# Thirty-two tiles in place of thirty-three for the routed experts of a decoder block, with other fixed experts

## The chip, the core and the metric

The kernel runs on one core of one Trainium2 chip. The metric is the device time of one execution, in microseconds (us). The core has a matrix engine (PE, with its weight loads as PEld), a vector engine (DVE), a scalar engine (ACT), a general engine (POOL) and SyncE (SP), which here issues nearly all transfers (DMAs). PSUM is the memory that PE writes.

## What is computed

One layer of a decoder block on 512 tokens of width 1024, in float32: two attention mixers with gates and an output projection, and behind them a mixture of 64 experts (each 1024 to 256 to 1024, SwiGLU), six experts for each token, and one shared expert. The part that matters here:

```python
_, expert_idx = lax.top_k(jnp.where(expert_keep, choice, NEG_INF), TOP_K)      # 6 of 64 for each token
def expert_block(xs):
    tok, g, e = xs
    xb = x_pad[tok]
    hb = jax.nn.silu(xb @ w_exp_gate[e]) * (xb @ w_exp_up[e])
    return (hb @ w_exp_down[e]) * g[:, None]
routed = jax.ops.segment_sum(yb.reshape(n_rows, D), row_tok, num_segments=T + 1)[:T]
shared = (jax.nn.silu(xf @ w_sh_gate) * (xf @ w_sh_up)) @ w_sh_down
return (shared + routed).reshape(B, S, D)
```

512 tokens with six experts each are 3072 rows of work for the 64 experts. How many an expert gets is known only once the router has run; for the inputs used it lies between 12 and 98.

## The kernel before

**Up to the router.** The norms, the projections, the two attentions, the merge and the output projection fill the first half of the span. The weights of four routed experts whose number is fixed beforehand (experts 0 to 3, `E0 = 4`) and of the shared expert are loaded in that time. `route`, `place` and `scatter` write for each expert a list of its tokens into a table in device memory. Then the experts other than the fixed four are ranked by how many rows they have (`krow`, `kcol` and `rowk` are the keys; the fixed ones get a large number added so that they rank first, in order of their number), and `sched` holds the expert of each rank.

**Units and tiles.** A rank has a fixed room of so many units of 32 rows, listed in `UNITS`; an expert with more rows than its rank's room goes into a loop at the very end (`For_i` over `n_over`), which does not run for these inputs. `make_layout` packs the units into tiles of four units, which is 128 rows: 132 units in 33 tiles before. An entry (q) of the layout is an expert in the order of use; it may straddle two tiles. The fixed experts have three units each and share tiles 0 to 3 with one small expert each; tile 31 has four experts and a piece, tile 32 four of one unit each.

**The work of one tile T** on PE, in the order written by hand: `first` (name `gu`, line 1266 before) multiplies the 128 rows by the gate and up weights of each expert of the tile, in halves of 64 rows where all pieces are even, else in quarters of 32 rows; `turn` (`tp`, line 1253) transposes the gathered rows of a later tile; `turn_hidden` (`tp<-hid`, line 1281); `expert_out` (`y`, line 1298) multiplies by the down weights; `combine` (`o`, lines 1322 and 1323) adds the rows to the tokens' sums `acc` through a matrix of zeros and ones, for two tiles at a time. The order in the loop is gate and up of tile T+1, transpose of tile T+2, combine of a finished pair where there is one, down of tile T. With 33 tiles the first combine takes tile 0 alone, with 32 the first one takes tiles 0 and 1.

**The queue of transfers.** There are six slots for an expert's weights: gate and up together as `gu`, down as `dn`, three transfers of 1024 KB. SP issues in program order and waits at each transfer until its slot is free. `tile_ents(T)` is called two tiles ahead of the down of T and asks for the slots' lists (`load_slots`, `tb`, nine entries ahead), the gate and up of each expert of the tile (`load_gu`), and behind each of them the down of the expert two entries earlier (`next_dn`, `DLAG = 2`). `fetch` on POOL gathers the rows of a tile (`xg`, `hs`) by its list. For the last tile the gate and up come as asked for and the downs last, in half pieces.

**The entry** into this stage is the string `ENTRY`: e, g, u and d load an expert's number, gate, up and down, s its list, f gathers a tile.

Of the kernel before, what the change touches and what calls it, by code (L numbers as in the profile page):

```python
# [10 lines left out]
F32 = mybir.dt.float32  # L11
# [6 lines left out]
ALU = mybir.AluOpType  # L18
# [20 lines left out]
EARLY = 1  # L39
SPL = (4, 7)  # L40
PW = {0: 3, 1: 3}
ENTRY = "e1 g1 u1 d1 s0 s1 f0 s2 s3 f1 s4 s5 s6 s7 s8 e3 g3 u3"
BYACT, HALVES = 1, 2
MODS, GST, MODE = 2, 8, ["vvvvvvvv"] * 4

# [1 line left out]

E0 = 4  # L50
UNITS = [3] * E0 + [4] + [3] * 9 + [2] * 39 + [1] * 11


def make_layout():
    small = [r for r in range(E0, 64) if UNITS[r] == 1]
    big = [r for r in range(E0, 64) if UNITS[r] > 2]
    mid = [r for r in range(E0, 64) if UNITS[r] == 2]
    head = [r for e in range(E0) for r in (e, small.pop(0))]
    spread = []
    for group in (big, mid):  # L60
        spread += [((i + 0.5) / len(group), r) for i, r in enumerate(group)]
    ranks = head + [r for _, r in sorted(spread)] + small
    layout, at = [], 0
    for r in ranks:
        pieces, left = [], UNITS[r]
        while left:
            n = min(left, 4 - at % 4)
            pieces.append((at // 4, at % 4, n, UNITS[r] - left))
            at, left = at + n, left - n
        layout.append((r, pieces))  # L70
    assert at % 4 == 0
    return layout, at // 4


LAYOUT, TILES = make_layout()
# [12 lines left out]
def build(ctx, tc, a, out, dbg=None):  # L88
# [594 lines left out]
    late = []  # L683
# [18 lines left out]
    def load_expert(slot, e, parts=1, now=True, after=None):  # L702
        gu = slots[slot][0].tile([128, 2, KD, 256], F32, name="gu", tag=f"gu{slot}")
        dn = slots[slot][1].tile([128, 2, D], F32, name="dn", tag=f"dn{slot}")
        if e is None:
            for j, n in enumerate(("w_sh_gate", "w_sh_up")):
                SP.dma_start(gu[:, j], a[n][0].rearrange("(p k) f -> p k f", k=KD))
            SP.dma_start(dn, a["w_sh_down"][0].rearrange("(b p) n -> p b n", p=128))
            return gu, dn
        moves = []  # L710
        if after is not None:
            for to in (gu[0:1, 0, 0, 0:1], gu[0:1, 1, 0, 0:1], dn[0:1, 0, 0:1]):
                A.copy(to, after[0:1, 0:1])
        for k in range(0, KD, KD // parts):
            for j, src in enumerate((wegv, weuv)):
                v = src[e].rearrange("o (p k) f -> (o p) k f", k=KD)
                moves.append((gu[:, j, k:k + KD // parts], v[:, k:k + KD // parts]))
        moves.append((dn, wedv[e].rearrange("o (p j) n -> (o p) j n", j=2)))
        for to, src in moves:
            if now:  # L720
                SP.dma_start(to, src)
            else:
                late.append(lambda to=to, src=src: SP.dma_start(to, src))
        return gu, dn
# [55 lines left out]
    ast.close()  # L780
    fst.close()
    slots.append([pool("wpd", 1, side="right")] * 2)
    WT[fixed[0]] = load_expert(2, slice(0, 1), now=False)

    owv = a["w_out"][0].rearrange("(k p) n -> p k n", p=128)
    wpb = pool("wpb", 1, side="right")
# [24 lines left out]
    for b in range(KD):  # L811
# [6 lines left out]
        V.tensor_tensor(gates[0][b], gates[0][b], gates[1][b], ALU.add)  # L818
        for j, (H, L) in enumerate(mg):
            split(H[:, b], L[:, b], gates[0][b][:, j * 256:j * 256 + 256], A, G)  # L820
    WT[fixed[1]] = load_expert(1, slice(1, 2), now=False)
    wst.close()
    omst.close()
    gst.close()
# [131 lines left out]
    def score_sum(i):  # L956
        lg = mm_p.tile([128, S], F32, name="lg", tag="mm")
        PE.matmul(lg[:, :NE], scores[i], pairs, start=True, stop=True)
        sc = rt.tile([128, NE], F32, name="sc", bufs=2)
        A.activation(sc, lg[:, :NE], AF.Exp, scale=-1.0)  # L960
        scores[i] = sc
        return sc
# [108 lines left out]
    for c in (1, 0):  # L1071
        out_raw(c)
        chunks[c] = out_split(c)
    WT[fixed[2]] = load_expert(3, slice(2, 3))
    lo, hi = range(0, 4), range(4, 8)
    norm_rows(0)
    norm_rows(1)
# [31 lines left out]
    shared_in(0, 1, 0, hi)  # L1109


    WT[fixed[3]] = load_expert(4, slice(3, 4), after=score_sum(3))
    SP.dma_start(gfb, bc(modd[5 * D:6 * D]))
    shared_in(0, 1, 1)
    place(2)
# [6 lines left out]

    krow = rt.tile([128, NE], F32, name="krow")
    V.tensor_scalar(krow, iota_e, -1.0, float(NE - 1), op0=ALU.mult, op1=ALU.add)
    V.tensor_scalar(krow[:, 0:E0], krow[:, 0:E0], 1e6, None, op0=ALU.add)
    kcol = rt.tile([128, 1], F32, name="kcol")
    G.tensor_scalar(kcol, ecol, -1.0, float(NE - 1), op0=ALU.mult, op1=ALU.add)
    G.tensor_scalar(kcol[0:E0], kcol[0:E0], 1e6, None, op0=ALU.add)
    cr = tr_p.tile([128, S], F32, name="cr", tag="tr")
    cc = cr[:, NE:]  # L1130
    for i in range(NT):
# [80 lines left out]

    def load_slots(q):
        rank, pieces = LAYOUT[q]
        o = rank * STRIDE if rank < E0 else SP.value_load(sched[0:1, 1, rank:rank + 1], min_val=0,
                                                          max_val=(NE - 1) * STRIDE)
        for T, u, n, r in pieces:
            src = table[o + r * 32:o + (r + n) * 32] if rank < E0 else table[ds(o + r * 32, n * 32)]
            SP.dma_start(tb[u * 32:(u + n) * 32, T], src)
# [131 lines left out]
    for step, q in ((t[0], int(t[1])) for t in ENTRY.split()):  # L1351
# [13 lines left out]
            SP.dma_start(gu[:, j], (wegv, weuv)[j][e].rearrange("o (p k) f -> (o p) k f", k=KD))  # L1365
        elif step == "d":
            WT[q][1] = load_dn(where[q], entry[q][1])
    late.append((3, entry[3][1]))
    follow(G.iota(iota_t, pattern=[[1, S]], base=0, channel_multiplier=0), last[0])

    def turn_next(T, parts):
# [186 lines left out]
```

## Time and profile before

| what | value |
|---|---|
| median of 3 runs | 1053.76 us (1049.55 to 1054.71) |
| the profiled execution's own time | 1039.41 us |
| its span, first to last instruction | 1037.6 us |
| mean granted clock of PE | 0.986 |
| PE busy | 999.0 us (96%) |
| DVE busy | 579.4 us (56%) |
| bytes moved | 285.98 MB, mean 276 GB/s |

The profiled execution is 14.35 us below the median of the runs. A busy PE is not PE at its peak, since ends of matmuls are modelled; its idle time and what ended it are what is to be read. Times in the trace are us from the start of the span. "L1266" is a line of the kernel.

### The profile page before, as it was taken

To read this page: it belongs to the slowest core of one execution; us is meant where nothing else is said; L and a number is where in the kernel's file an instruction comes from. 1 tells how busy PE (TensorE), PEld (TensorE's weight loads), DVE (VectorE), ACT (ScalarE), POOL (GpSimd) and SP (SyncE) were. 2 spreads that over 40 slices of the span, in tenths; PEclk is the share of its full clock that TensorE was granted. 3 is DMA by queue.
4 is the path that set the end of the run, shared out by engine and by line. 5 is a ranking of instruction groups with operands and counts; after the bars stand their busy time and mean duration, and the time that the engine had idled before them with its cause. 6 is when DMAs were issued, how large, how long until landed. Compare 5 with 4: busy or idle time off the path is not lost.

```text
span 1037.6 us, 16324 instructions
## 1 busy us (share of the span) xinstructions
PE 999.0 (96%) x5904; PEld 600.2 (58%) x5904; DVE 579.4 (56%) x1157; ACT 319.1 (31%) x712; POOL 158.3 (15%) x208
## 2 busy tenths in 40 slices
PE   9989999998989999999899999999999999999995
PEld 7778667776756668986334344444344444345442
DVE  4568576466757654595254455454455454445465
ACT  4356553232225532430122212122212122212213
POOL 2242001000031275135200000000000000000001
PEclk9999999999999999999999999999999999999998
DMA  9922104599660277635599999999999999999973
GB/s 296 321 86 65 45 1 155 193 282 271 187 211 21 82 263 236 232 104 227 208 415 415 417 416 371 377 418 412 389 378 374 378 408 417 383 366 418 379 264 143
DMA packets 101347, 285.98 MB, mean 276 GB/s; under 512 B 15121, under 2 KB 61929, under 8 KB 77202
## 3 DMA queue, kind: packets, MB, share of 16 engines
q1 hardware_dynamic: 94146, 270.18, 70.2%
q0 software_dynamic: 5648, 12.63, 3.2%
q10 hardware_dynamic: 1472, 2.11, 0.7%
q8 instruction: 47, 0.77, 0.3%
q14 instruction: 34, 0.28, 0.1%
HBM read 282.33 MB, written 4.66 MB: 277 GB/s over the span
## 4 chain that ended last, share of the span: by engine, by line
PE 79%; DVE 7%; DMA 6%; POOL 3%; issue 2%; ACT 2%; SPq 1%; ACTq 0%; POOLq 0%; DVEq 0%
PE gu L1266 22%; PE y L1298 11%; PE o L151 6%; PE o L1322 6%; PE o L150 6%; PE o L152 6%; PE o L1323 6%; PE tp L1253 3%; PE sp L591 3%; PE oc L615 2%; PE tp L603 2%; POOL table L1027 1%; PE tp L1281 1%; DMA w<-in_w_mod_dram 1%; POOL wL L159 1%
## 5 line engine op out<-in xcount | busy, mean ns | idle before, releaser
L1266 PE MATMUL gu<-gu,xT 128*32 128x512 f32 (+1 forms) x1664 | 233.6, 594 | 0.0
L1266 PEld LDWEIGHTS gu<-gu,xT 128*32 128x32 f32 (+1 forms) x1664 | 69.1, 117 | 150.4 <-issue 137.0
L1298 PE MATMUL y<-dn,hid 128*32 128x512 f32 (+1 forms) x832 | 120.3, 596 | 0.5 <-ACT hid L1282 0.5
L1275 DVE TENSOR_TENSOR hid<-hid,gu 128x256 f32<-128x256 f32 x33 | 13.9, 420 | 164.3 <-ACT hid L1274 164.3
L1322 PE MATMUL o<-yH,oht 128*128 128x512 f32 x260 | 103.9, 400 | 0.7 <-DVE acc L1324 0.7
L1324 DVE TENSOR_TENSOR acc<-acc,o 128x512 f32<-128x512 f32 x140 | 93.2, 683 | 17.3 <-PE o L1323 17.3
L1323 PE MATMUL o<-yL,oht 128*128 128x512 f32 x260 | 101.7, 391 | 0.0
L150 PE MATMUL o<-hH,wH 128*128 128x512 f32 x208 | 83.4, 401 | 1.2 <-ACT gate L473 1.2
L151 PE MATMUL o<-hH,wL 128*128 128x512 f32 x208 | 83.1, 399 | 1.5 <-DVE wL L159 1.4
L152 PE MATMUL o<-hL,wH 128*128 128x512 f32 x208 | 82.5, 396 | 0.0
L156 ACT CAST yH<-ys 128x512 fp32r<-128x512 f32 (+1 forms) x68 | 41.1, 605 | 106.3 <-DVE ys L1302 106.3
L159 DVE TENSOR_TENSOR yL<-ys,yH 128x512 fp32r<-128x512 f32 (+1 forms) x68 | 45.8, 676 | 43.3 <-ACT yH L156 43.2
L1298 PEld LDWEIGHTS y<-dn,hid 128*32 128x32 f32 (+1 forms) x832 | 32.7, 117 | 64.3 <-issue 54.2
L1274 ACT ACTIVATE hid<-gu 128x256 f32<-128x256 f32 x33 | 12.7, 384 | 185.2 <-PE gu L1266 185.2
L1302 DVE SCALAR_TENSOR_TENSOR ys<-y,tb,gmb 128x512 f32<-128x512 f32 (+1 forms) x68 | 49.8, 734 | 27.6 <-PE y L1298 24.2
L1241 POOL DMA_INDIRECT xg<-h2d,tb x22 | 22.2, 1009 | 274.4 <-PE tp L1253 196.8
L1322 PEld LDWEIGHTS o<-yH,oht 128*128 128x128 f32 x260 | 48.8, 188 | 14.9 <-DVE acc L1324 2.6
L1323 PEld LDWEIGHTS o<-yL,oht 128*128 128x128 f32 x260 | 48.9, 188 | 9.5
L919 ACT ACTIVATE xT<-tp,ab 128x128 f32<-128x128 f32 x132 | 49.6, 456 | 14.6 <-PE tp L1253 13.0
L921 DVE TENSOR_SCALAR xT<-tp,ab 128x128 f32<-128x128 f32 x132 | 45.2, 404 | 10.9 <-ACT xT L919 7.4
L150 PEld LDWEIGHTS o<-hH,wH 128*128 128x128 f32 x208 | 39.5, 190 | 13.2 <-issue 1.9
L151 PEld LDWEIGHTS o<-hH,wL 128*128 128x128 f32 x208 | 39.6, 190 | 10.9 <-DVE wL L159 3.0
(386 smaller groups left out, 1669.1 us busy)
## 6 DMA issues: line engine op xcount, KB each, us to landing
gu<-in_w_exp_gate_dram SPq DMA_DIRECT2D x63, 1024.0 KB, 8.6
gu<-in_w_exp_up_dram SPq DMA_DIRECT2D x63, 1024.0 KB, 13.1
dn<-in_w_exp_down_dram SPq DMA_DIRECT2D x60, 1024.0 KB, 10.9
w<-in_w_mod_dram SPq DMA_DIRECT2D x32, 512.0 KB, 3.8
w<-in_w_in_dram SPq DMA_DIRECT2D x13, 1024.0 KB, 8.0
wm<-in_w_mod_dram SPq DMA_DIRECT2D x16, 512.0 KB, 7.1
wraw<-in_w_out_dram SPq DMA_DIRECT2D x12, 512.0 KB
dn<-in_w_exp_down_dram SPq DMA_DIRECT2D x8, 512.0 KB, 8.9
```

The source lines that it names most:

```text
L150: PE.matmul(o, l[0], r[0], start=start, stop=False)
L151: PE.matmul(o, l[1], r[0], start=False, stop=False)
L152: return PE.matmul(o, l[0], r[1], start=False, stop=stop)
L159: return le.tensor_tensor(L, src, f(H), ALU.subtract)
L919: A.activation(out, src, AF.Identity, bias=ab2[:, 1, k:k + 1], scale=ab2[:, 0, k:k + 1])
L921: V.tensor_scalar(out, src, ab2[:, 0, k:k + 1], ab2[:, 1, k:k + 1], op0=ALU.mult, op1=ALU.add)
L1266: last[0] = PE.matmul(gu[lo:lo + n], xT[:, k, lo:lo + n], w[:, :, k], start=(k == 0), stop=(k == KD - 1))
L1298: last[0] = PE.matmul(y[lo:lo + m], hT[:, j, lo:lo + m], w[:, j, c], start=(j == 0), stop=(j == 1))
L1302: V.scalar_tensor_tensor(ys[:, b], y[:, b], f(tb[:, T, 1:2]), gfb[:, c][:, b], op0=ALU.mult, op1=ALU.mult)
L1322: m = PE.matmul(o, oht[:, i * 128:(i + 1) * 128], yH[:, c], start=(q == 0), stop=False)
L1323: PE.matmul(o, oht[:, i * 128:(i + 1) * 128], yL[:, c], start=False, stop=(q == len(state) - 1))
L1324: d = V.tensor_tensor(acc[:, i, c], acc[:, i, c], o, ALU.add)
```

## The change

Three of the four parts stand in tables. `UNITS` gives the four fixed experts two units in place of three, keeps one rank of four units, has ten ranks of three, 37 of two and twelve of one, in sum 128 units. `make_layout` no longer lets an expert straddle tiles: tiles 0 and 1 hold the four fixed experts alone, two each; the others hold two experts of two units, or one of three and one of one; in the middle the one expert of four units has tile 16 alone, and behind it tile 17 holds three experts (two units and twice one). The fixed experts are numbers 4 to 7 (`FIX`), with the keys and addresses that follow from it. `ENTRY` is written anew: entries 4 and 5 are now the first to be loaded behind the ranking, and gate and up of the second stand behind six lists in place of nine. The room of experts 4 to 7 is 64 rows each; they get 63, 52, 41 and 56.

```diff
--- before.py
+++ after.py
@@ -39,7 +39,7 @@
 EARLY = 1
 SPL = (4, 7)
 PW = {0: 3, 1: 3}
-ENTRY = "e1 g1 u1 d1 s0 s1 f0 s2 s3 f1 s4 s5 s6 s7 s8 e3 g3 u3"
+ENTRY = "e4 g4 u4 d4 s0 s1 f0 s2 s3 f1 s4 s5 e5 g5 u5 s6 s7 s8"
 BYACT, HALVES = 1, 2
 MODS, GST, MODE = 2, 8, ["vvvvvvvv"] * 4
 
@@ -47,29 +47,31 @@
 
 
-E0 = 4
-UNITS = [3] * E0 + [4] + [3] * 9 + [2] * 39 + [1] * 11
+
+E0, FIX = 4, 4
+UNITS = [2] * E0 + [4] + [3] * 10 + [2] * 37 + [1] * 12
 
 def make_layout():
-    small = [r for r in range(E0, 64) if UNITS[r] == 1]
-    big = [r for r in range(E0, 64) if UNITS[r] > 2]
-    mid = [r for r in range(E0, 64) if UNITS[r] == 2]
-    head = [r for e in range(E0) for r in (e, small.pop(0))]
-    spread = []
-    for group in (big, mid):
-        spread += [((i + 0.5) / len(group), r) for i, r in enumerate(group)]
-    ranks = head + [r for _, r in sorted(spread)] + small
-    layout, at = [], 0
-    for r in ranks:
-        pieces, left = [], UNITS[r]
-        while left:
-            n = min(left, 4 - at % 4)
-            pieces.append((at // 4, at % 4, n, UNITS[r] - left))
-            at, left = at + n, left - n
-        layout.append((r, pieces))
-    assert at % 4 == 0
-    return layout, at // 4
+    of = lambda n: [r for r in range(E0, 64) if UNITS[r] == n]
+    four, three, two, one = of(4), of(3), of(2), of(1)
+    kinds = [[(r, one.pop(0)) for r in three], [(two[i], two[i + 1]) for i in range(0, len(two) - 1, 2)]]
+
+
+    spread = [tile for _, tile in sorted(((i + 0.5) / len(group), tile) for group in kinds
+                                         for i, tile in enumerate(group))]
+    odd = [tuple(four), (two[-1], one.pop(0), one.pop(0))]
+    half = len(spread) // 2
+    tiles = [(e, e + 1) for e in range(0, E0, 2)] + spread[:half] + odd + spread[half:]
+    assert len([r for t in tiles for r in t]) == 64
+    layout = []
+    for T, ranks in enumerate(tiles):
+        at = 0
+        for r in ranks:
+            layout.append((r, [(T, at, UNITS[r], 0)]))
+            at += UNITS[r]
+        assert at == 4
+    return layout, len(tiles)
 
 LAYOUT, TILES = make_layout()
@@ -780,7 +782,7 @@
     ast.close()
     fst.close()
     slots.append([pool("wpd", 1, side="right")] * 2)
-    WT[fixed[0]] = load_expert(2, slice(0, 1), now=False)
+    WT[fixed[0]] = load_expert(2, slice(FIX + 0, FIX + 1), now=False)
 
     owv = a["w_out"][0].rearrange("(k p) n -> p k n", p=128)
     wpb = pool("wpb", 1, side="right")
@@ -818,7 +820,7 @@
         V.tensor_tensor(gates[0][b], gates[0][b], gates[1][b], ALU.add)
         for j, (H, L) in enumerate(mg):
             split(H[:, b], L[:, b], gates[0][b][:, j * 256:j * 256 + 256], A, G)
-    WT[fixed[1]] = load_expert(1, slice(1, 2), now=False)
+    WT[fixed[1]] = load_expert(1, slice(FIX + 1, FIX + 2), now=False)
     wst.close()
     omst.close()
     gst.close()
@@ -1071,7 +1073,7 @@
     for c in (1, 0):
         out_raw(c)
         chunks[c] = out_split(c)
-    WT[fixed[2]] = load_expert(3, slice(2, 3))
+    WT[fixed[2]] = load_expert(3, slice(FIX + 2, FIX + 3))
     lo, hi = range(0, 4), range(4, 8)
     norm_rows(0)
     norm_rows(1)
@@ -1109,7 +1111,7 @@
     shared_in(0, 1, 0, hi)
 
-    WT[fixed[3]] = load_expert(4, slice(3, 4), after=score_sum(3))
+    WT[fixed[3]] = load_expert(4, slice(FIX + 3, FIX + 4), after=score_sum(3))
     SP.dma_start(gfb, bc(modd[5 * D:6 * D]))
     shared_in(0, 1, 1)
     place(2)
@@ -1122,10 +1124,14 @@
 
     krow = rt.tile([128, NE], F32, name="krow")
     V.tensor_scalar(krow, iota_e, -1.0, float(NE - 1), op0=ALU.mult, op1=ALU.add)
-    V.tensor_scalar(krow[:, 0:E0], krow[:, 0:E0], 1e6, None, op0=ALU.add)
+    V.tensor_scalar(krow[:, FIX:FIX + E0], krow[:, FIX:FIX + E0], 1e6, None, op0=ALU.add)
     kcol = rt.tile([128, 1], F32, name="kcol")
     G.tensor_scalar(kcol, ecol, -1.0, float(NE - 1), op0=ALU.mult, op1=ALU.add)
-    G.tensor_scalar(kcol[0:E0], kcol[0:E0], 1e6, None, op0=ALU.add)
+    kfix = rt.tile([128, 2], F32, name="kfix")
+    G.tensor_scalar(kfix[:, 0:1], ecol, FIX - 0.5, 1e6, op0=ALU.is_gt, op1=ALU.mult)
+    G.tensor_scalar(kfix[:, 1:2], ecol, FIX + E0 - 0.5, None, op0=ALU.is_lt)
+    G.tensor_tensor(kfix[:, 0:1], kfix[:, 0:1], kfix[:, 1:2], ALU.mult)
+    G.tensor_tensor(kcol, kcol, kfix[:, 0:1], ALU.add)
     cr = tr_p.tile([128, S], F32, name="cr", tag="tr")
     cc = cr[:, NE:]
     for i in range(NT):
@@ -1212,7 +1218,7 @@
 
     def load_slots(q):
         rank, pieces = LAYOUT[q]
-        o = rank * STRIDE if rank < E0 else SP.value_load(sched[0:1, 1, rank:rank + 1], min_val=0,
+        o = (FIX + rank) * STRIDE if rank < E0 else SP.value_load(sched[0:1, 1, rank:rank + 1], min_val=0,
                                                           max_val=(NE - 1) * STRIDE)
         for T, u, n, r in pieces:
             src = table[o + r * 32:o + (r + n) * 32] if rank < E0 else table[ds(o + r * 32, n * 32)]
@@ -1365,7 +1371,7 @@
             SP.dma_start(gu[:, j], (wegv, weuv)[j][e].rearrange("o (p k) f -> (o p) k f", k=KD))
         elif step == "d":
             WT[q][1] = load_dn(where[q], entry[q][1])
-    late.append((3, entry[3][1]))
+    late.append((5, entry[5][1]))
     follow(G.iota(iota_t, pattern=[[1, S]], base=0, channel_multiplier=0), last[0])
 
     def turn_next(T, parts):
```

On SP, behind the loads of the first ranked expert: `tb` are the lists, `TENSOR_LOAD sched` reads an expert's number for the next instructions, `gu` is a gate or up transfer. Before, the rows up to the first list of the second tile:

```order
L699 DMA dn<-in_w_exp_down_dram 128x2048
L1219 DMA tb<-table 96x2
L1215 TENSOR_LOAD sched
L1215 ISA x2
L1219 ISA
L1219 DMA tb<-table 32x2
L1219 DMA tb<-table 96x2
```

and now up to the second ranked expert's gate:

```order
L701 DMA dn<-in_w_exp_down_dram 128x2048
L1225 DMA tb<-table 64x2 x4
L1221 TENSOR_LOAD sched
L1221 ISA x2
L1225 ISA
L1225 DMA tb<-table 64x2
L1221 TENSOR_LOAD sched
L1221 ISA x2
L1225 ISA
L1225 DMA tb<-table 64x2
L1364 TENSOR_LOAD sched
L1364 ISA x2
```

The two lists of the first tile now follow each other with no number read between them, and six lists in all, not nine, stand ahead of the second expert.

On PE, from the transpose for tile 2 on: `y` is the down product, `o` the combine. Before:

```order
L1253 MATMUL tp<-ident,hs 128x128 x8
L1298 MATMUL y<-dn,hid 32x512 x16
L1281 MATMUL tp<-ident,hid 128x128 x2
L1266 MATMUL gu<-gu,xT 32x512 x32
L1253 MATMUL tp<-ident,xg_3470 128x128 x8
L1322 MATMUL o<-yH,oht 128x512
L1323 MATMUL o<-yL,oht 128x512
```

and now:

```order
L1259 MATMUL tp<-ident,hs 128x128 x8
L1304 MATMUL y<-dn,hid 64x512 x8
L1287 MATMUL tp<-ident,hid 128x128 x2
L1272 MATMUL gu<-gu,xT 64x512 x16
L1259 MATMUL tp<-ident,xg_3470 128x128 x8
L1304 MATMUL y<-dn,hid 64x512 x8
L1287 MATMUL tp<-ident,hid 128x128 x2
L1272 MATMUL gu<-gu,xT 32x512 x32
L1259 MATMUL tp<-ident,xg_3471 128x128 x8
L1328 MATMUL o<-yH,oht 128x512
L1329 MATMUL o<-yL,oht 128x512
```

The combine of tile 0 alone is gone; the next tile's down and gate and up stand in its place, and the first combine takes two tiles.

## Rows read from the trace of the kernel before

**Rows 1.** The page: the span in 40 equal slices of 25.9 us.

```profile
DMA  9922104599660277635599999999999999999973
GB/s 296 321 86 65 45 1 155 193 282 271 187 211 21 82 263 236 232 104 227 208 415 415 417 416 371 377 418 412 389 378 374 378 408 417 383 366 418 379 264 143
```

**Rows 2.** Waits of PE from 500 to 1005 us: total, times, longest.

```profile
PE tp L1281 <- DVE hid L1275: 1.5, 1, 1.5
PE o L1322 <- DVE acc L1324: 0.7, 1, 0.7
```

**Rows 3.** Stretches: length, PE, PEld, DVE, ACT, POOL busy, clock, DMA share, GB/s.

```profile
526.00:976.00 450.00, 449.34 (x2864) 206.56 (x2858) 223.95 (x409) 101.51 (x233) 32.54 (x54) 1.00 0.98 397
526.00:635.00 109.00, 108.34 (x664) 49.74 (x658) 55.20 (x101) 24.62 (x57) 8.43 (x14) 1.00 1.02 416
573.00:588.50 15.50, 15.50 (x86) 5.35 (x80) 6.86 (x12) 4.65 (x10) 1.21 (x2) 1.00 1.02 418
526.50:542.00 15.50, 14.84 (x112) 6.37 (x112) 9.05 (x17) 3.25 (x8) 1.21 (x2) 1.00 1.01 414
512.00:516.00 4.00, 2.47 (x26) 1.47 (x26) 1.69 (x5) 2.26 (x6) 1.20 (x2) 1.00 0.70 231
```

**Rows 4.** Timeline of PE, tiles 0 to 4: start, length, line, shapes, count, [idle].

```profile
498.85 1.59 PE L1253 MATMUL tp<-ident,xg 128*128 128x128 f32 x8 [1.68 <-DMA xg<-h2d,tb]
500.24 4.83 PE L1061 MATMUL so<-dn,hs 128*128 128x512 f32 x8
505.00 7.07 PE L1266 MATMUL gu<-gu,xT 128*32 128x512 f32 x64
...
526.96 7.07 PE L1266 MATMUL gu<-gu,xT 128*32 128x512 f32 x64
...
543.84 7.05 PE L1266 MATMUL gu<-gu,xT 128*32 128x512 f32 x64
```

**Rows 5.** Timeline of PE, halves of 64 rows in tiles 5 and 6.

```profile
574.92 7.09 PE L1266 MATMUL gu<-gu,xT 128*64 128x512 f32 x32
...
586.91 7.09 PE L1266 MATMUL gu<-gu,xT 128*64 128x512 f32 x32
```

**Rows 6.** Timeline of PE at the end: tiles 30 to 32.

```profile
959.71 7.07 PE L1266 MATMUL gu<-gu,xT 128*32 128x512 f32 x64
...
1000.61 3.64 PE L1298 MATMUL y<-dn,hid 128*32 128x512 f32 x32
...
1016.41 3.64 PE L1298 MATMUL y<-dn,hid 128*32 128x512 f32 x32 [0.46 <-ACT hid L1282]
```

**Rows 7.** Timeline of SP at the entry.

```profile
491.63 1.95 SPq L1219 DMA_DIRECT2D tb<-table  x3
...
492.78 0.33 SPq L1219 DMA_DIRECT2D tb<-table  x1
...
500.09 0.36 SPq L1365 DMA_DIRECT2D gu<-in_w_exp_gate_dram  x1
...
512.12 0.35 SPq L694 DMA_DIRECT2D gu<-in_w_exp_gate_dram  x1
```

**Rows 8.** Timeline of POOL near 395 us.

```profile
395.36 0.18 POOL L1127 TENSOR_SCALAR kcol<-ecol 128x1 f32<-128x1 f32 x1
...
403.53 1.18 POOL L915 TENSOR_TENSOR acc<-acc,tt 128x256 f32<-128x256 f32 x1 [6.01 <-DMA acc<-in_x_dram]
```

**Rows 9.** DMA from 440 us: issues (count, KB each, us to landing) and POOL's queue.

```profile
q0 software_dynamic: 5520, 12.62, 5.6%
...
gu<-in_w_exp_gate_dram SPq DMA_DIRECT2D x60, 1024.0 KB, 12.6
...
tb<-table SPq DMA_DIRECT2D x8, 0.8 KB, 1.8
```

**Rows 10.** Waits of SP's queue from 500 to 980 us.

```profile
SPq L699 <- PE y L1298: 150.8, 24, 11.1
SPq L694 <- PE gu L1266: 63.6, 22, 5.7
```

## The prediction

> **What bounds the kernel now.** I read the page's slices first. From slice 20 on (518 us) the transfers run at 415 to 418 GB/s for four slices and at 366 to 418 GB/s in most of the rest [rows 1]: half of the span is a stage of routed experts in which the transfers are nearly full. The waits of PE in this stage then say which of the two ends last: from 500 to 1005 us the longest wait is 1.5 us, on DVE, and not one is for weights [rows 2]. So PE sets the end, at clock 1.00. The stretches give the reserve of the other side [rows 3]: 416 GB/s from 526 to 635 us, in pieces of 15.5 us 414 to 418, but a mean of only 397 from 526 to 976. The dips are SP waiting for a slot: 150.8 us behind down products and 63.6 us behind gate and up [rows 10]. Weights arrive ahead of PE until the six slots are full, and then PE paces them. The reserve is 416 against 397, about 5%. That is to be held against the change, which takes work off PE and none off the transfers.
>
> **What the change takes off PE.** A tile fewer, and the combine of tile 0 alone. The two together are one step of the old sequence: gate and up of tile 2 begins at 526.96 us and of tile 3 at 543.84 us [rows 4], and the step between holds gate and up, transpose, the single combine and down. The new sequence lacks just this step: its tile n does from there on what the old tile n+1 did. Halves in place of quarters change nothing, 7.09 us against 7.07 for gate and up [rows 4, 5]. So PE loses **16.9 us**.
>
> **The entry.** PE's first transpose waits 1.68 us for the gather of tile 0 [rows 4], which needs two lists. The second went out at 492.78 us, 1.15 us after the first at 491.63; the third followed within 0.8 us of it, the static kind [rows 7]. Both lists of tile 0 are now static, so the second goes out about 0.7 us sooner. I take **0.7 us**, between 0 and the whole 1.68 of the wait. The gate and up of the second ranked expert go out some 3 us sooner than 500.09 us (three lists fewer ahead of them). This is worth nothing: tile 2 is its first user, at 526.96 us before, and the transfers stand idle in between anyway, since the next slot is freed by the gate and up of tile 0 (512.12 us [rows 7]). If that cover were missing, the gain would be those 3 us. The lists 6 to 8 queue behind them and come some 2 us later; the gathers that use them are due after 520 us.
>
> **The new key on POOL** is three instructions more of about 0.2 us, just ahead of a wait of 6.01 us for a transfer [rows 8]: nothing. Without that wait it would be 0.6 us.
>
> **The transfers.** Now the same 60 experts must come in while PE runs a step less. Two tiles take PE 31.1 us (tile 6 to tile 30, 12 pairs: from 586.91 to 959.71 us is 372.8 us [rows 5, 6]). They need four experts of three loads of 1024 KB (1.0486 MB), so 12.58 MB, and two gathers, a sixteenth of POOL's 12.62 MB [rows 9], 0.79 MB: 13.37 MB, at 416 GB/s 32.1 us. The transfers fall behind by 1.0 us a pair. Whether this reaches PE is a sum from the start.
>
> Start: SP's first load that waits for tile 0 goes out at 512.12 us; the window 512 to 516 holds 231 GB/s, 0.92 MB or 2.2 us at full rate [rows 3, 7], so bytes flow from 513.8, now from 513.1 us. Landing adds about 1.8 us, the time of the smallest list load [rows 9], an estimate. The tightest point is the last odd tile but one, tile 29 (experts 58 and 59; the tail behind it leaves more room). Up to it pass: gate and up of experts 6 to 59, 54 x 2 x 1.0486 = 113.2 MB; downs 5 to 56, which is 52 x 1.0486 = 54.5 MB; gathers of 28 tiles, 28/32 of 12.62 = 11.0 MB. In sum 178.7 MB, at 416 GB/s 429.6 us. The weights are there at 513.1 + 429.6 + 1.8 = 944.5 us. PE wants them where the old tile 30 began, 959.71 - 16.9 - 0.7 = 942.1 us. PE waits **2.4 us**, in pieces of under 1 us at the odd tiles from about tile 21 on. At 418 GB/s (427.5 us) it would wait 0.3 us, at 414 (431.6 us) 4.4 us.
>
> Tile 16 with one expert and tile 17 with three are four experts in two tiles like any pair; the slots let two of the three be fetched under tiles 14 to 16, so I cost them at nothing (without that cover an expert is 3.15 MB or 7.6 us). The last tile with two experts in place of four needs four late half loads fewer, but the last down product waited 0.46 us for ACT and not for a load [rows 6]: nothing.
>
> **Sum:** 16.9 + 0.7 - 2.4 = 15.2 us. The profiled execution's own 1039.41 us become 1024.2 us, a span of 1022.4; taken off the median of the runs, 1053.76, which stands 14.35 us above for a reason that the trace doesn't show, **1038.6 us**. With the rates from 414 to 418 and the ends of the entry (0 to 1.7), this forecast runs from 1035.5 to 1041.5.
>
> **Rivals.** *Hidden after all:* the rate holds at 418 or the lead is larger, and PE never waits: 17.6 us, 1036.2. For it speaks that PE was fed at full rate up to 635 us without a wait. Against it speaks the lag of 1.0 us a pair.
>
> *The transfers become the bound:* all hangs on the rate, 1 GB/s being 1.0 us (178.7 MB at 415 is 430.6 us). At 402 GB/s the sum up to tile 29 is 444.5 us, the wait 17.3, and the gain is gone; from there on the kernel is slower. The old one isn't yet slower there, since its mean need is 397. At 390 GB/s the sum is 458.2 us, the weights of tile 29 are there at 973.1 us, PE waits 31.0 us, and the end is 13.4 us later than before, at 1067.2 us. For it: the runs' median lies 14.35 us over the profiled execution, and if this gap lies in the transfers, this case is here. Against it: 414 is the lowest piece of the full stretch.
>
> The Trainium skill (HBM Reference, Specifications) gives a core about 358 GB/s when both cores of a pair stream and about 425 alone. By the trace, 416 GB/s, this core was alone, and no run here shows the other case; by 358 the sum to tile 29 would be 499 us, an estimate, and the kernel slower.
>
> *Between the two:* 404 to 411 GB/s, a wait of 7 to 15 us, 1044 to 1051 us.
>
> *The experts don't fit:* one of experts 4 to 7 with over 64 rows would start the loop at the end, a load of 7.6 us and a tile of 12 us at least, over 1058 us. The fullest has 63 rows; against it speaks the count.
>
> **How the numbers follow.** Forecast 0.50, hidden after all 0.16, between 0.18 (half of it within 5.3 us of before), transfers as the bound 0.15, of which 0.04 stay within 5.3 us, experts don't fit 0.01. About 0.5%, 5.3 us, is what a measurement of this kernel can tell from no change. Faster by more: 0.50 + 0.16 + 0.09 = 0.75. Within: 0.09 + 0.04 = 0.13. Slower: 0.12. The range leaves out the slower cases and the upper part of those within, in all under 0.2, and reaches from 1034.5, below the hidden case with the whole entry wait, to 1052.
>
> **What would show it.** PE's gate and up of tile 3 begins straight behind the down of tile 1, 12.0 us after tile 2's, as tile 6 behind tile 5 before [rows 5]; the old step of 16.9 us is not there. Between 526 and 950 us the transfers run at 414 to 418 GB/s with no dips, where the mean was 397, and SP's waits behind down products fall from 150.8 us to a fraction, replaced by waits on its own loads. PE shows waits for weights, each under 1 us at odd tiles, in sum 0.3 to 4.4 us. A sum over 10 us, waits before tile 15, a wait at tile 17 of several us, or a rate below 410 would show the forecast wrong; so would dips with PE waiting, which would mean that slots and not the rate hold the loads back.

## The result, and the profile after

The changed kernel takes 1041.5 us (1039.2 to 1044.0, 6 runs), the kernel before beside it 1050.1 (1047.9 to 1054.7, 6 runs): a ratio of 0.9927 [0.9906, 0.9948], or 8.6 us less (5.5 to 9.9 by the interval). The forecast was 1038.6 us and 15.2 us less. The sign held, and the time lies in the range, though at the upper end of the forecast's own bounds (1035.5 to 1041.5); of the gain 6.6 us are missing. That the time comes within 2.9 us of the forecast is in part luck: the forecast was taken off a median of before of 1053.76 us (3 runs), and over six runs that median is 1050.1. A second and a third set of runs, on other chips, gave 0.9940 [0.9918, 0.9962] and 0.9919 [0.989, 0.9948].

The page of the changed kernel, the span in 40 slices of 26 us; [rows 1] are the same lines of before:

```profile
DMA  9932104599660277713689999999999999999932
GB/s 287 312 97 68 48 0 152 189 279 277 185 212 21 81 262 240 249 62 133 225 336 415 417 415 417 416 416 415 417 410 417 415 414 417 411 417 418 411 120 82
```

The dips to 366 to 389 of [rows 1] are gone: the transfers run at 410 to 418 GB/s in every slice from 547 to 990 us. PE's timeline, gate and up of tiles 0 to 3 (start, length, line, shapes, count):

```profile
519.40 7.09 PE L1272 MATMUL gu<-gu,xT 128*64 128x512 f32 x32
529.41 7.09 PE L1272 MATMUL gu<-gu,xT 128*64 128x512 f32 x32
541.40 7.09 PE L1272 MATMUL gu<-gu,xT 128*64 128x512 f32 x32
553.39 7.07 PE L1272 MATMUL gu<-gu,xT 128*32 128x512 f32 x64
```

Tile 3 follows 12.0 us behind tile 2; the step of 16.9 us of [rows 4] is gone, as forecast. The waits of SP's queue from 500 to 980 us (total, times, longest), against [rows 10]:

```profile
SPq L701 <- DMA dn<-in_w_exp_down_dram: 103.2, 46, 3.4
SPq L696 <- DMA gu<-in_w_exp_up_dram: 100.1, 50, 3.1
...
SPq L701 <- PE y L1304: 7.3, 6, 3.5
```

SP used to wait 150.8 us for PE to free a slot. Now that is 7.3 us (and 11.2 in place of 63.6 behind gate and up), and it waits for its own earlier loads. PE no longer paces the transfers. PE's waits from 500 to 1005 us, against [rows 2]:

```profile
PE tp L1259 <- DMA xg<-h2d,tb: 5.0, 1, 5.0
PE gu L1272 <- DMA gu<-in_w_exp_up_dram: 2.2, 2, 1.9
PE tp L1287 <- DVE hid L1281: 1.5, 1, 1.5
```

The 2.2 us for weights seem to sit right on the forecast's 2.4. They are not the whole wait. The ends of matmuls are modelled, and part of a wait can be counted as busy time. The starts of the tiles tell more. From tile 3 to tile 15 the step from the start of an odd tile's gate and up to the next tile's is 19.0 to 19.2 us. From tile 17 to tile 27 these steps grow to 19.4, 22.0, 19.6, 19.8, 20.5 and 19.9, and that behind tile 29 is 22.6 where 21.6 is regular. The longest is that of tile 19; its gate and up starts, waits, goes on, and tile 20 follows:

```profile
802.14 1.06 PE L1272 MATMUL gu<-gu,xT 128*32 128x512 f32 x6
805.10 7.05 PE L1272 MATMUL gu<-gu,xT 128*32 128x512 f32 x58 [1.90 <-DMA gu<-in_w_exp_up_dram]
824.10 7.04 PE L1272 MATMUL gu<-gu,xT 128*64 128x512 f32 x32
```

The step is 2.9 us too long, and the row of waits has 1.9 of them. The granted clock is 1.00 from 790 to 950 us, so a lower clock doesn't explain the rest. The group of gate and up shows the same in one row; after the bar stand busy us, mean ns of one, and idle us with its cause:

```profile
L1272 PE MATMUL gu<-gu,xT 128*32 128x512 f32 (+1 forms) x1376 | 232.1, 594 | 2.2 <-DMA gu<-in_w_exp_up_dram 2.2
```

and in a version of it in which weights can't be late (it loads half of each down weight, experiments below):

```profile
L1272 PE MATMUL gu<-gu,xT 128*32 128x512 f32 (+1 forms) x1376 | 226.6, 594 | 0.0
```

Busy and idle together are 234.3 us against 226.6 for the same 1376 matmuls: **PE waits 7.7 us for weights**. Two more profiles of the changed kernel give 9.2 and 7.9 in this way. (In the first of these 1.7 us are a lower clock in the last tile but one, told at the end.)

One warning on these two profiles. The span of the profiled execution after is 1042.2 us, longer than that of before, 1037.6. The difference arose ahead of the changed stage, in work that the change leaves alone. ACT's copy before the last scores of the router, after:

```profile
470.00 0.27 ACT L955 COPY lgT<-lg 128x128 f32<-128x128 f32 x1 [9.12 <-remote]
```

Before, it ran at 461.02 us after 0.89 us of idle. This idle time comes and goes in both kernels (next section), so the stage is compared from the first gate and up on.

### The profile page after: what moved, and what is told of

The parts are those of the page before. It is cut to its first block, busy times and chain, and to the rows that moved or that the text cites. A ratio compares the mean times of both kernels' runs of the same rounds, so it can differ in the third digit from the quotient of the medians.

```text
span 1042.2 us, 15330 instructions
## 1 busy us (share of the span) xinstructions
PE 990.4 (95%) x5446; PEld 600.8 (58%) x5446; DVE 570.2 (55%) x1139; ACT 315.6 (30%) x704; POOL 156.1 (15%) x209
## 4 chain that ended last, share of the span: by engine, by line
PE 48%; DMA 37%; DVE 6%; POOL 2%; ACT 2%; issue 2%; another core or an unknown queue 1%; SPq 1%; ACTq 0%; POOLq 0%; DVEq 0%
DMA gu<-in_w_exp_up_dram 31%; PE gu L1272 8%; PE o L153 5%; PE o L152 5%; PE o L154 5%; PE y L1304 4%; PE sp L593 3%; PE oc L617 2%; DMA w<-in_w_mod_dram 2%; PE o L1328 2%; PE o L1329 2%; PE tp L605 2%; PE og L1050 1%; PE so L1063 1%
## 5 line engine op out<-in xcount | busy, mean ns | idle before, releaser
L1272 PEld LDWEIGHTS gu<-gu,xT 128*32 128x32 f32 (+1 forms) x1376 | 72.2, 123 | 148.1 <-issue 131.7
L1304 PE MATMUL y<-dn,hid 128*32 128x512 f32 (+1 forms) x688 | 116.8, 597 | 0.5 <-ACT hid L1288 0.5
L1328 PE MATMUL o<-yH,oht 128*128 128x512 f32 x252 | 100.1, 397 | 0.0
L1329 PE MATMUL o<-yL,oht 128*128 128x512 f32 x252 | 98.5, 391 | 0.0
L1330 DVE TENSOR_TENSOR acc<-acc,o 128x512 f32<-128x512 f32 x132 | 88.4, 684 | 17.4 <-PE o L1329 17.4
L153 PEld LDWEIGHTS o<-hH,wL 128*128 128x128 f32 x208 | 39.5, 190 | 11.8 <-DVE wL L161 3.9
```

Source lines behind the costliest of these rows:

```text
L153: PE.matmul(o, l[1], r[0], start=False, stop=False)
L1272: last[0] = PE.matmul(gu[lo:lo + n], xT[:, k, lo:lo + n], w[:, :, k], start=(k == 0), stop=(k == KD - 1))
L1304: last[0] = PE.matmul(y[lo:lo + m], hT[:, j, lo:lo + m], w[:, j, c], start=(j == 0), stop=(j == 1))
L1328: m = PE.matmul(o, oht[:, i * 128:(i + 1) * 128], yH[:, c], start=(q == 0), stop=False)
L1329: PE.matmul(o, oht[:, i * 128:(i + 1) * 128], yL[:, c], start=False, stop=(q == len(state) - 1))
L1330: d = V.tensor_tensor(acc[:, i, c], acc[:, i, c], o, ALU.add)
```

## The experiments

All ratios are against runs of the kernel before on the same chip. The runs came in three sets on three chips: the first four kernels below, the next four, the last four.

**Is the late router part of the change?** Both kernels, unchanged.

> The kernel before, unchanged, for a second profile. In the first profile of the changed kernel PE's work stands 10.5 us later than in the profile of before between the scores of the last 128 tokens and the shared expert (461 to 471 us), with ACT idle for 9.12 us at one copy. Theory A, the delay comes and goes by itself and the first profile of before lacked it: a profile of this run shows an idle time of ACT of several us at the same place, its first gate and up of tile 0 begins at 512 to 520 us in place of 505.0, and its own time is 1047 to 1055 us. Theory B, the change causes the delay: gate and up of tile 0 begins at 505 +- 1 us again, and the own time is 1038 to 1041 us.

> The changed kernel again, for a second profile and a second interval against before. Theory A (the delay at 461 us comes and goes): the time is 0.990 to 0.995 of before, and the profile may or may not have the idle time of ACT; if it lacks it, gate and up of tile 0 begins near 505 us. Theory B (the change causes it): the idle time of ACT is there again and gate and up of tile 0 begins at 519 +- 1 us. Both: the steps between gate and up of tiles 18 to 31 hold about 7 us more than the steps of 12.0 and 19.1 us, as in the first profile.

Measured: 0.9995 [0.9976, 1.0014] and 0.9940 [0.9918, 0.9962]. The idle time at the same copy was 4.65 us in the kernel before (at 461.15 us) and 6.11 in the changed one (at 464.13):

```profile
461.15 0.27 ACT L953 COPY lgT<-lg 128x128 f32<-128x128 f32 x1 [4.65 <-remote]
```

So it isn't caused by the change, and theory A holds, if not in all its numbers: gate and up of tile 0 began at 506.66 us in the kernel before, where it expected 512 to 520, and at 511.13 in the changed one. On the other two chips all profiles show 0.9 us.

**Is the rate of the transfers what holds the gain back?** Half of each ranked down weight isn't loaded, and the product takes the loaded half in its place, so PE's work stays the same. The edit is the same in both kernels; its load:

```
-        SP.dma_start(dn, wedv[e].rearrange("o (p j) n -> (o p) j n", j=2))
+        SP.dma_start(dn[:, 0], wedv[e].rearrange("o (p j) n -> (o p) j n", j=2)[:, 0])
```

> The changed kernel with half of each ranked expert's down weights left out (the first of its two parts is loaded and used for both), so 0.52 MB of 3.15 MB less for each of 60 experts; PE's work is the same. Theory R, the transfers' rate holds PE back by 7 to 8 us from tile 17 on: these waits vanish, steps are 12.0 and 19.1 us to the end, and the time is 7 to 8 us (0.7%) below the changed kernel's. Rival S, the slots and SP's waits hold PE back and not the bytes: the waits stay and the time is within 2 us of the changed kernel's.

> The kernel before with the same half of the down weights left out. In both theories PE sets its pace, so the time stays within 2 us of before. If it falls by 5 us or more, the kernel before was held back by transfers in the timed runs though not in its profile, and the gap of 14 us between its profile and its runs lies there.

Measured: 0.9855 [0.9808, 0.9903] for the changed kernel and 0.9988 [0.9967, 1.0009] for the one before. The stretch from 526 to 976 us of the changed kernel so cut (length, busy PE, PEld, DVE, ACT and POOL, clock, DMA share, GB/s):

```profile
526.00:976.00 450.00, 449.68 (x2650) 207.00 (x2648) 219.93 (x401) 102.53 (x234) 32.66 (x54) 1.00 0.92 358
```

and of the kernel before, so cut:

```profile
526.00:976.00 450.00, 449.34 (x2878) 205.32 (x2876) 223.54 (x409) 103.08 (x237) 33.88 (x56) 1.00 0.86 336
```

With a sixth of the expert bytes gone, the changed kernel needs only 358 GB/s and PE is busy throughout. From the first to the last gate and up it takes 482.0 us, the kernel before 499.0: the 16.9 us are there in full (17.0). With all its bytes the changed kernel takes 491.2 on this chip, 9.2 us more, of which 1.7 are the lower clock. The intervals of the two ratios, with half of the down weights and with all, don't overlap. Theory R holds.

**Does it matter that the tile of three experts stands in the middle?** It goes to the last place.

```
-    ... + spread[:half] + odd + spread[half:]
+    ... + spread[:half] + odd[:1] + spread[half:] + odd[1:]
```

> The changed kernel with the tile of three experts moved from place 17 to the last place; nothing else. Tiles 17 to 30 then need one expert (3.15 MB, 7.6 us at 416 GB/s) less up to their start. Theory T (the transfers fall 1 us a pair behind PE, and the odd tile in the middle brings the crossing 7.6 us forward): the waits at gate and up of tiles 18 to 30, 6.4 to 6.9 us by the steps of the two profiles of the changed kernel and 9.2 with the last two tiles, shrink to under 1 us, and the time falls by 6 to 9 us against the changed kernel, to a ratio of about 0.986 to 0.988 against before. Theory M (the bytes of the whole stage at 412 GB/s set the end, wherever the tile stands): the waits only move to the last tiles, and the time changes by less than 2 us.

Measured: 0.9842 [0.9815, 0.9869], 16.6 us less than before. The group of gate and up:

```profile
L1272 PE MATMUL gu<-gu,xT 128*32 128x512 f32 (+1 forms) x1376 | 226.7, 594 | 0.0
```

and the stretch from 526 to 950 us:

```profile
526.00:950.00 424.00, 424.00 (x2487) 195.30 (x2484) 206.69 (x376) 95.78 (x220) 31.33 (x52) 1.00 1.02 416
```

No wait is left, though the transfers still run at 416 GB/s. They don't end sooner: the last weight load goes out 474 us behind the start of tile 0's gate and up, 472 in the third profile of the changed kernel. What changed is that the extra expert isn't needed until the last tile. Theory T holds, M falls. The gain against the changed kernel, 8 to 10 us by the ratios, is above the 6 to 9 that T gave; no unchanged copy of the changed kernel ran on this chip. On the third chip the tile was moved with another edit held (the last two runs below), and that is 6.7 us, 1032.7 to 1026.0, with intervals that don't overlap.

**Did the second ranked weights, queued sooner, delay tile 0?** PE's first transpose waits longer for its gather than before (5.0 us against 1.68 in [rows 4]), and these 2 MB were queued beside that gather.

```
-ENTRY = "e4 g4 u4 d4 s0 s1 f0 s2 s3 f1 s4 s5 e5 g5 u5 s6 s7 s8"
+ENTRY = "e4 g4 u4 d4 s0 s1 f0 s2 s3 f1 s4 s5 s6 s7 s8 e5 g5 u5"
```

> The changed kernel with gate and up of the second ranked expert queued behind all lists again, as before the change; nothing else. Theory E (those 2 MB run beside the gather of tile 0, PE waits longer for it and goes on at the lower clock): the wait of the first transpose returns from 3.1 (5.0 in the other profile) to between 1.1 and 1.7 us, the clock there stays at 1.00, gate and up of tile 0 begins some 11.7 us after the first list instead of 14.2 to 18.8, and the time falls by 2.5 to 4.5 us against the changed kernel. Theory P (tile 0 is late since the router's part ahead of it is late in some executions): the distance from first list to gate and up stays, and the time changes by under 1 us; or, if the earlier start helps the transfers, rises by 2.5 us.

> The changed kernel with both edits: the tile of three experts last, and the second ranked weights behind all lists. If theories T and E hold and their parts are separate, the gains add up: 9 to 13 us less than the changed kernel, a ratio of 0.981 to 0.985 against before. Under theories M and P it stays within 2 us of the changed kernel. If only one holds, it equals the run that has that one.

The reverse edit in the kernel before (the second ranked weights ahead of the last three lists):

> The kernel before with one part of the change: gate and up of the second ranked expert queued ahead of the last three lists. Here PE and not the transfers sets the end, so what tile 0 loses is lost. Theory E: the first transpose waits 1.5 to 4 us longer, the clock drops behind it, and the time rises by 2 to 4.5 us, a ratio of 1.002 to 1.004. Theory P, and the prediction's own step: 0, a ratio of 1.000.

Measured: 0.9902 [0.9879, 0.9925]; both edits 0.9865 [0.9837, 0.9893], no better than the tile alone; and 0.9996 [0.9973, 1.002] in the kernel before. Theory E falls, at least as a cost of microseconds. In the edited kernel before PE did wait longer for the gather, 3.74 us, but gate and up of tile 0 began 13.4 us behind the first list, as in the kernel before. With the weights behind the lists again, PE of the changed kernel still waited 2.4 us:

```profile
PE tp L1259 <- DMA xg<-h2d,tb: 2.4, 1, 2.4
```

What does differ is the gather. The first list goes out 7.2 to 7.3 us ahead of PE's first transpose in the four profiles of the kernel before and its variants, and 7.7 to 8.0 in eight of ten of the changed one and its variants (with the edit, without it, and with the tile moved), 9.2 and 12.1 in two. The gather of tile 0 takes 3.4 us from issue to landing in the kernel before (DMA issues in a window around it: count, us to landing):

```profile
xg<-h2d,tb POOLq DMA_INDIRECT x1, 3.4
```

and 4.3 in the kernel with the tile moved:

```profile
xg<-h2d,tb POOLq DMA_INDIRECT x1, 4.3
```

POOL's queue moves 0.59 MB for the gathers of tiles 0 and 1 before (packets, MB, share of the engines' time):

```profile
q0 software_dynamic: 288, 0.59, 43.1%
```

and 0.87 MB in the changed kernel with the weights behind the lists:

```profile
q0 software_dynamic: 288, 0.87, 38.7%
```

Both are 288 packets. The new first tiles hold two static experts of 64 rows each and are nearly full: the four have 212 rows, which at 4 KB each are the 0.87 MB. The old tiles had more empty places, and these cost next to no bytes. 0.28 MB more are 0.7 us at 416 GB/s, an estimate. This reading is by the two rows; no run changed the rows of tile 0 alone.

Behind the first transpose the clock adds to this. Ahead of tile 0's gate and up stands a product of the shared expert, here in the second profile of the kernel before and in the third of the changed one:

```profile
503.13 3.60 PE L1061 MATMUL so<-dn,hs 128*128 128x512 f32 x8
503.06 4.96 PE L1063 MATMUL so<-dn,hs 128*128 128x512 f32 x8
```

In the second of these PE had just waited 4.3 us for the gather, and the granted clock from 500 to 504 us was 0.50, which is 1.2 GHz; in the first it had waited 1.55 us, and the clock was 1.00 there. Of the four profiles of the kernel before and its variants two have the short product and two a longer one (4.83 and 5.30 us); the ten of the changed one and its variants all have a longer one (4.1 to 5.2 us). From the first list to gate and up of tile 0 it is 11.7 to 11.8 and 13.4 us in the former and 14.1 to 14.5 in eight of the latter (15.1 and 18.8 in the two). So the new entry costs 0.7 to 2.8 us, by the execution.

**Is it the place of the tile, or the bytes up to the last tiles?** The changed kernel once more, and three edits on the third chip: the tile of three at place 25, the down of the second ranked expert loaded ahead of tile 0, and this with the tile at the end.

> The changed kernel unchanged, beside the next three on one chip. Both theories: 0.992 to 0.995 against before, waits of 6 to 9 us at gate and up of tiles 18 to 31. If the gain here is 10 us as in the run with the second ranked weights behind the lists, that edit did nothing and only the chip differed; if it is 5 to 8 us, the edit may be worth 2 to 4.

Measured: 0.9919 [0.989, 0.9948], 6.7 us less than before, with 7.9 us of waits. The interval overlaps that of the run with the second ranked weights behind the lists, so no effect of that edit is shown.

```
-    ... + spread[:half] + odd + spread[half:]
+    ... + spread[:half] + odd[:1] + spread[half:half + 8] + odd[1:] + spread[half + 8:]
```

> The changed kernel with the tile of three experts at place 25 in place of 17; nothing else. Theory N (only the number of experts needed up to the last tiles counts, for the transfers run at their rate all the while): the waits of tiles 18 to 24 vanish and one wait of 4 to 7 us stands at tiles 25 to 27, the sum up to tile 29 stays at 6 to 7 us, and the time within 2 us of the changed kernel's. Theory D (the tile disturbs the order of slots where it stands, and each tile behind it pays): the waits fall to the share of tiles behind place 25, about 3 us, and the time by 3 to 4 us.

Measured: 0.9947 [0.993, 0.9964], a median 1.1 us above the changed kernel's beside it, with intervals that overlap. All steps up to tile 24 are regular. Then PE's timeline, gate and up of tile 25, first part and rest:

```profile
881.26 1.06 PE L1272 MATMUL gu<-gu,xT 128*32 128x512 f32 x6
888.59 8.81 PE L1272 MATMUL gu<-gu,xT 128*32 128x512 f32 x58 [6.28 <-DMA gu<-in_w_exp_up_dram]
```

One lump in place of six small waits. The step took 28.1 us where 19.1 is regular: 9.0 us, of which 6.28 are the wait and the rest the slower matmuls behind it (8.81 us for 58 of them; a full 64 take 7.07), at a granted clock of 0.50 in the next 4 us:

```profile
888.00:892.00 4.00, 3.41 (x16) 0.80 (x20) 0.00 (x0) 0.00 (x0) 0.00 (x0) 0.50 1.01 414
```

Behind tile 25 no tile waits. Theory N holds, with the lump larger than it said; D falls.

> The changed kernel with the down of expert 5 (1.05 MB, 2.5 us at 416 GB/s) loaded ahead of tile 0, where the transfers stand idle, in place of behind the gate and up of tile 0. Theory N: the stream of the stage is 2.5 us shorter, every wait of PE for weights together falls by 2.5 us, and so does the time. If waits for slots and not bytes set the pace, 0.

(In `ENTRY` this is a `d5` at the end, in place of the line `late.append((5, entry[5][1]))`.) Measured: 0.9938 [0.9917, 0.9959], and 231.7 + 2.5 us in gate and up, 7.6 us of waits: nothing gained. The reason is in SP's timeline. The changed kernel:

```profile
515.06 0.37 SPq L696 DMA_DIRECT2D gu<-in_w_exp_gate_dram  x1
```

and this one:

```profile
508.43 0.36 SPq L701 DMA_DIRECT2D dn<-in_w_exp_down_dram  x1
509.59 8.16 SPq L1225 DMA_DIRECT2D tb<-table  x7
518.58 0.37 SPq L696 DMA_DIRECT2D gu<-in_w_exp_gate_dram  x1
```

The down waits 3.9 us for the shared experts' product to free its slot; behind it in SP's queue stand seven lists of 8.16 us together, and the first load that waits for tile 0 goes out 10.3 us behind the start of that tile's gate and up (508.33 us), where it was 7.1 (from 507.95). The 2.5 us won were given back in the queue. Theory N isn't refuted, but this run didn't test it.

> The tile of three experts last and the down of expert 5 early. With the tile last PE had no wait for weights left, so by theory N the 2.5 us that the transfers gain here are worth nothing: the ratio of the run with the tile last alone, 0.984 to 0.987. If the transfers still hold PE back where the profile shows no wait, 1 to 2.5 us less than that.

Measured: 0.9880 [0.9855, 0.9904], not better than the tile moved alone (0.9842 [0.9815, 0.9869], on another chip); its profile has 1.7 us of the lower clock near the end. The best version of the study is the one with only the tile of three experts last: one line's edit, with a ratio 0.008 to 0.010 below those of the changed kernel; its two variants lie 0.004 to 0.0075 below.

## Why the prediction was right, and where it was off

- *PE loses one step, 16.9 us:* right. 17.0 us between the two kernels with half the down bytes, and 16.6 measured in the time once the waits are out of the way (tile of three last; the interval is wide, 13.6 to 19.2).
- *POOL's key, the halves in place of quarters:* no run separated them, and the sum below has no need of them.
- *The entry, 0.7 us sooner:* wrong in sign. PE's first transpose stands some 0.7 us later behind the first list, and gate and up of tile 0 0.7 to 2.8 us later, the lower clock included. The gathers behind the lists move 0.28 MB more, the likely cause, which no run tested alone. I priced the lists and neither what they fetch nor the clock behind the wait. That the second ranked weights are worth nothing was right (0.9996 in the kernel before).
- *The transfers as the pace-maker from the middle on:* right in kind. SP's waits for PE vanished, the rate held at 414 to 418 GB/s for most slices, the waits came at the odd tiles, from tile 17 on where the forecast said about 21, and one of them was 2.9 us where it said under 1.
- *PE waits 2.4 us:* this is the term that was off; 7.7 were measured. My sum put the weights of tile 29 at 513.1 + 429.6 + 1.8 = 944.5 us. SP's first load that waits for tile 0 would by the same forecast have gone out at 511.4 (512.12 before, 0.7 sooner), so that is 433.1 us behind it, and PE was to want them 430.7 us behind it. In the third profile of the changed kernel this load goes out at 515.06. Gate and up of tile 29 begins at 951.94 and stops after two matmuls, until the tile's last weight is in:

```profile
951.94 1.07 PE L1272 MATMUL gu<-gu,xT 128*64 128x512 f32 x2
953.49 7.05 PE L1272 MATMUL gu<-gu,xT 128*64 128x512 f32 x30 [0.48 <-DMA gu<-in_w_exp_up_dram]
```

  The chain that ended last has the load of this weight (issue, us to landing):

```profile
932.75 20.60 DMA gu<-in_w_exp_up_dram
```

  So it was in at 953.35 us, 438.3 us behind the first gated load, 5.2 later than forecast. The row of the stretch, and what SP's queue moved in it (packets, MB, share):

```profile
515.06:953.45 438.39, 434.96 (x2532) 198.67 (x2532) 210.23 (x386) 100.04 (x230) 33.88 (x56) 1.00 1.01 414
q1 hardware_dynamic: 27192, 170.14, 94.6%
```

  My count of loads stands: up to the last weight of tile 29 SP issued just the 160 loads that I had, 167.8 MB. But its queue had moved 170.1 MB by then, and all queues together 181.3 where my sum for tile 29 was 178.7. These 2.6 MB are 6.3 us at 414 GB/s, against the 1.8 us that I allowed for landing: 4.5 us. The rate with the slow start in it gives most of the rest: 178.7 MB at 414 are 431.6 us, against 429.6 and the 1.7 allowed for the start, and by the unrounded rate (181.3 MB in 438.4 us) 0.4 us more. PE itself would have begun tile 29 some 430.5 us behind that load, by the profile with half of the down weights. So the wait is 7.9 us in this profile, and 7.7 and 7.5 in the others, in which PE went on 438.2 and 437.9 us behind the load. A landing of 1.8 us, read from the smallest list load [rows 9], was the wrong row. Weight loads have their own: 12.6 us from issue to landing before [rows 9], and now (count, KB, us to landing, 526 to 950 us)

```profile
dn<-in_w_exp_down_dram SPq DMA_DIRECT2D x53, 1024.0 KB, 22.4
gu<-in_w_exp_gate_dram SPq DMA_DIRECT2D x53, 1024.0 KB, 17.0
gu<-in_w_exp_up_dram SPq DMA_DIRECT2D x53, 1024.0 KB, 19.9
```

  At 2.5 us of bytes each, some seven to nine loads are on their way at a time, an estimate, and parts of later ones are in before an earlier one is whole. Why the later loads were just 2.4 MB ahead, the trace doesn't tell, since it doesn't keep which of the 16 engines moved a packet; this stays open.
- *The tail behind tile 29 leaves more room:* right. The step behind tile 29 took 22.6 to 23.2 us, against 21.6 where no weight is late, but this is the wait inside tile 29's own gate and up (above). With the 6.4 us of the tiles up to it, these 1.5 make up the 7.9 of the third profile. The step behind tile 30 is 22.8 us with late weights and without (24.5 in profiles with the lower clock).
- *Tile 17 with three experts at nothing:* right for tile 17 itself, which waits 0.4 us at most, but the wrong question. My sum for tile 29 contained the extra expert, and I never asked what the sum would be without it. It is 7.6 us less, and then no tile waits. That was the most valuable line of the change, and it stood in the forecast as a zero.
- *Sum:* -17.0 + 7.7 + 0.7 = -8.6 us, and 8.6 were measured; that it comes out to the tenth is luck, with an interval of 5.5 to 9.9 and an entry of 0.7 to 2.8. Of the 6.6 us that are missing against the forecast, 5.3 are the wait and 1.4 the entry. On the other chips 6.4 and 6.7 were measured; the waits there are 7.5 (without the lower clock) and 7.9, and the upper end of the entry makes the sums -6.7 and -6.3. How often an execution has which entry isn't known from single profiles.
- *Rivals:* the rate stayed, so neither "transfers become the bound" nor "hidden after all" came; the wait of 7.7 us lies at the near end of "between the two", but not from a lower rate. The Trainium skill (HBM Reference, Specifications) puts a core alone at about 425 GB/s. The 416 that the transfers hold here while their queue is full agrees, and the case of both cores of a pair was not run.

## What to carry to other kernels

When two resources are within some per cent of each other, write down the demand of the weaker one as a running sum up to each tile, and look for the tile that brings it forward. Here a tile that needs more weights than the others did best at the end, behind which nothing waits. In such a sum, price the landing by the load that is waited for, at the number of loads then on their way, and not by a small load. Waits of PE for an operand can hide in its busy time (2.2 us of 7.7 were shown as waits here); compare the same group's busy plus idle between two kernels, or the steps between tiles.

## What the runs showed of the hardware

- In five of fourteen profiles, of both kernels, the granted clock falls near the last tiles, and the gate and up of the last tile but one then takes 1.7 us more (a step of 24.5 us against 22.8). PE has a wait of only 0.3 us just ahead of it, which the profiles without the fall have too. The kernel with the tile at place 25:

```profile
974.00:978.00 4.00, 4.00 (x24) 1.03 (x26) 0.16 (x1) 0.58 (x1) 0.00 (x0) 0.57 1.01 398
```

  and the same place in the changed kernel beside it:

```profile
975.00:979.00 4.00, 4.00 (x41) 1.22 (x44) 0.36 (x1) 0.70 (x2) 0.00 (x0) 1.00 1.00 399
```

  0.57 is a mix of the two levels, 1.2 and 2.4 GHz: 24 matmuls against 41 in 4 us. What makes it fall isn't shown.
- The gather's empty places are packets, but hardly bytes: 288 packets were 0.59 MB in one kernel and 0.87 in the other. Over the whole stage before, POOL's queue moved 12.62 MB [rows 9]: 3072 rows of 4 KB are 12.58, and 33 full tiles would be 17.3.
- In three of four profiles on one chip, and in the first profile of the changed kernel, ACT stood still for 4.7 to 9.1 us at the same instruction, released by nothing that the profile names, with PE and DVE behind it; POOL went on. Both kernels show it, and its cause stays open. It is as large as the whole effect of the change, which is why two single profiles can't be set against each other by their spans.
